# One 32-column strip of the array per quarter of a unit's columns: the decode rows of an input projection on one core

## The chip, the cores and the metric

The kernel runs on one core of a Trainium2 chip. The metric is the device time of one execution in microseconds (us). The core has TensorE (PE, with its weight loads shown apart as PEld), VectorE (DVE), ScalarE (ACT), GpSimd (POOL) and SyncE (SP, which here only issues transfers). The chip grants TensorE a clock that can be lower than the full one; the profile lists the granted share.

## The reference, cut to what matters

A two-branch decoder layer is computed for a prompt of 1024 tokens and, with the same weights, for 8 decode tokens (`x_sample`, one token in each of 8 sequences). What the change touches is the input projection of those 8 rows:

```python
D_MODEL, SEQ, DEC_BATCH = 1024, 1024, 8
SPLIT_SIZES = (W_A, W_A, W_B, W_B, W_B, W_B, W_B, H_B, H_B)     # 7 x 1024 columns, then 2 x 4

def hybrid_layer(x, ...):
    hn = rmsnorm(x, g_norm)
    u = hn @ w_in                                               # (rows, 1024) @ (1024, 7176)
    xa, za, uq, uk, uv, uo, zb, ui, uf = jnp.split(u, SPLIT_IDX, axis=-1)
    k = uk.astype(jnp.float32).reshape(B, S, H_B, DK) * (DK ** -0.5)    # 1/16
    ...

y_prompt, ... = trunk(x_prompt, zero states, weights)           # 1024 rows
y_sample, ... = trunk(x_sample, given states, weights)          # 8 rows
```

## The kernel before, in words

The 7168 wide columns of `w_in` are taken in 14 units of 512 columns, two groups of 256 each (`UNITS`: v0v1, x0y0, q0k0 and so on). A unit's weights lie in two tiles, `raws[u, 0]` for the first 512 rows of `w_in` and `raws[u, 1]` for the last 512, each as 128 partitions x 4 blocks x 512 columns; the 8 blocks of 128 rows are the "blocks of k". `blk(u, a, b)` is the half `a` (256 columns) of tile `b`. `load_raw` fetches a tile in two transfers of 512 KB on SP's queue, one for each half; the next unit's tile goes into the same buffer, so its transfers wait for the last reader of the old one.

For the prompt each unit is multiplied in seven products (a fast scheme on 2x2 blocks, `Q_P1` to `Q_P7`), each of 24 or 48 matmuls, written by `mm3` (lines 66 to 68) as three matmuls on halves of the numbers. These fill TensorE. `prep` makes the operands of a product two products ahead: ScalarE rounds (line 72), VectorE subtracts (line 73). Unit 0 has no such products: its 8 row tiles go through `plain`, while the prompt's rows are still being normalised and transposed (line 442).

The 8 decode rows are multiplied apart, once for each unit, by `dec_unit` (line 251). Its stationary operand is a window of 32 columns of `hnd`: the 8 normalised decode rows of one block of k, transposed, and 24 columns more that nobody reads. Only 32 of the array's 128 columns are needed, and so the array is used as four strips of 32 columns, strip g writing the PSUM partitions 32g to 32g+31. Block k goes to strip k mod 4 and streams all 512 columns of the unit (line 256). Each strip thus holds a partial sum over two blocks of k. ScalarE copies the 128x512 result to `Z` (line 259). Some steps later `turn` transposes its four 128x128 pieces on TensorE (line 264), and VectorE adds the four partial sums while it picks the 8 real rows (line 267), and scales those of a k group by 1/16 (line 269).

A plain float32 matmul is issued as two passes, each with a weight load of its own; so the 8 matmuls of a unit are 16 records in the profile. I call the run of a unit's matmuls its burst.

`dec_unit` is called by `prep` when a unit's fifth-block product (`Q_P5`) is prepared, ahead of the two VectorE steps that overwrite the raw tile in place (lines 281 and 282), and for unit 0 on line 583. Which instruction stands where on an engine is worked out when the kernel is built: a scheduler orders each engine's instructions by its own estimate of when they can start, and each engine then runs its list strictly in that order. For units 0 and 1 the result lies in the PSUM tile `ps_tr`, of which there is one; for the others in `ps_o`, of which there are three.

Of the kernel before, what the change touches and what calls it, by code (L numbers as in the profile page):

```python
# [13 lines left out]
ALU = mybir.AluOpType  # L14
# [3 lines left out]
P = 128  # L18
T = 1024
HT = 512  # L20
NB = 8
KC = 8
# [29 lines left out]
def hymba_kernel(  # L52
# [7 lines left out]
    V, A, G, TE = nc.vector, nc.scalar, nc.gpsimd, nc.tensor  # L60
# [21 lines left out]
    def ps(tag, shape):  # L82
        return psp.tile(shape, F32, tag=tag, name=f"ps_{tag}", bufs=NBUF.get(tag, 1))

    def const(shape, name, dt=F32):
        return cpool.tile(shape, dt, tag=name, name=name)
# [14 lines left out]
    def sg(shape, name, dt=F32):  # L101

        return stg.tile(shape, dt, tag="stg", name=name)
# [4 lines left out]
    def dconst(shape, name):  # L108

        return dpool.tile(shape, F32, tag=name, name=name)  # L110


    idF = const([P, P], "idF")
# [33 lines left out]
    hnd = dconst([P, KC * NB + 24], "hnd")  # L147
# [84 lines left out]
    raws = {}  # L232

    def load_raw(u, b, parts=(0, 1)):
# [5 lines left out]
        for a in parts:  # L240
# [5 lines left out]
    dec_dst = {"q": lambda j: dqk[:, 0, 2 * j:2 * j + 2], "k": lambda j: dqk[:, 1, 2 * j:2 * j + 2],  # L246
               "v": lambda j: dqk[:, 2, 2 * j:2 * j + 2], "o": lambda j: do[:, 2 * j:2 * j + 2],
               "z": lambda j: dz[:, 2 * j:2 * j + 2], "x": lambda j: dxz[:, 0, 2 * j:2 * j + 2],
               "y": lambda j: dxz[:, 1, 2 * j:2 * j + 2]}

    def dec_unit(u):

        pz = ps("tr" if u < 2 else "o", [P, 512])
        for k in range(KC):
            g = k % 4
            TE.matmul(pz[32 * g:32 * g + 32, :], hnd[:, NB * k:NB * k + 32], raws[u, k // 4][:, k % 4, :], start=k < 4, stop=k >= 4,  # L256
                      skip_group_check=True)
        Z = sg([P, 512], "Z")
        A.copy(Z, pz)

        def turn():
            pt = ps("tr", [P, 4, P]) if u < 2 else pz.rearrange("p (m q) -> p m q", m=4)
            for m in range(4):
                TE.transpose(pt[:, m, :], Z[:, m * P:(m + 1) * P], idF)  # L264
            for a, (kind, j) in enumerate(units[u]):
                src = pt[:, 2 * a:2 * a + 2].rearrange("p m (g b) -> p m b g", g=4)[:, :, 0:NB, :]
                V.tensor_reduce(dec_dst[kind](j), src, axis=mybir.AxisListType.X, op=ALU.add)
                if kind == "k":
                    V.tensor_scalar(dec_dst[kind](j), dec_dst[kind](j), 1.0 / 16.0, None, op0=ALU.mult)
        late.append(turn if u < 2 else lambda: late.append(turn))  # L270


# [2 lines left out]
    def blk(u, a, b):  # L275
        return raws[u, b][:, :, a * 256:(a + 1) * 256]

    def prep(u, q):
        if q == Q_P5:
            dec_unit(u)  # L280
            V.tensor_tensor(blk(u, 0, 0), blk(u, 0, 0), blk(u, 1, 0), op=ALU.subtract)
            V.tensor_tensor(blk(u, 1, 0), blk(u, 1, 0), blk(u, 1, 1), op=ALU.add)
        if q == Q_P6:
            V.tensor_tensor(blk(u, 1, 0), blk(u, 1, 1), blk(u, 0, 0), op=ALU.subtract)
        src = {Q_P1: (0, 0), Q_P2: (0, 1), Q_P5: (1, 0), Q_P6: (1, 0), Q_P7: (0, 0), Q_P3: (0, 1), Q_P4: (1, 1)}
        hi, lo = ws([P, 4, 256], f"wh{u}_{q}"), ws([P, 4, 256], f"wl{u}_{q}")
        split(hi, lo, blk(u, *src[q]))
        wops[u, q] = hi, lo
        if q == Q_P6:
            V.tensor_tensor(blk(u, 0, 1), blk(u, 0, 1), blk(u, 1, 0), op=ALU.subtract)  # L290
        b = {Q_P7: 0, Q_P4: 1}.get(q)
        if b is not None:
            if u + 1 < len(units):
                load_raw(u + 1, b)
            else:
                if b == 1:
                    r_open(0)
# [229 lines left out]
    kind, j = units[0][0]  # L527
# [53 lines left out]
    V.tensor_tensor(gd, pgd[0:NB], bgate[0:NB], op=ALU.add)  # L581
    ld(d_gd, gd)
    dec_unit(0)
    load_raw(1, 0)
    load_raw(1, 1)
# [387 lines left out]
    def decode_steps(h):  # L973
# [13 lines left out]
        def token(b):  # L987
# [18 lines left out]
            def products():  # L1006
# [10 lines left out]
                if b == NB - 1:  # L1017
                    Z = sg([P, 256], "qC")
                    V.tensor_copy(Z, pq[:, 0:256])

                    def turn():
                        pt = pq[:, 256:272].rearrange("p (v b) -> p v b", v=2)
                        for vb in range(2):
                            TE.matmul(pt[:, vb, :], Z[:, vb * P:(vb + 1) * P], selq, start=True, stop=True)
                        V.tensor_copy(dqC[:, 2 * h:2 * h + 2, :], pt)
# [803 lines left out]
```

## Time and profile before

| what | value |
|---|---|
| median of 3 runs | 916.23 us (916.17 to 916.24) |
| span of the profiled execution, first to last instruction | 913.5 us |
| its own time beside the span | not listed apart; the median of the runs is 2.7 us above the span |
| mean granted TensorE clock | 0.998 |
| PE, PEld busy | 902.1 us (99%), 749.2 us (82%) |
| DVE, ACT, POOL busy | 741.5 us (81%), 590.1 us (65%), 194.2 us (21%) |
| moved by DMA | 167.68 MB, mean 184 GB/s |
| matmul records | 5259, of them 224 on line 256 and 56 on line 264 |

How to read it: times in the tables below are us from the start of the span; a row of the timeline gives start, length to the end of the last of the merged instructions, engine, line, operation, the tiles out<-in, the part of the array (rows*columns), the shape streamed and the count. Matmuls overlap their neighbours, so how often they start matters more than how long one lasts.

### The profile page before, as it was taken

The page shows a single profiled execution, that of the slowest core. Times are in us where ns is not written, and L with a number is a line of the kernel's source. Part 1 is how long each engine was busy: PE and PEld are TensorE (multiplying, and loading weights), DVE is VectorE, ACT ScalarE, POOL GpSimd, SP SyncE. Part 2 cuts the span into 40 slices and gives each one's busy share as a digit, 9 for nine tenths or more (in the row PEclk, how much of TensorE's full clock was granted, in tenths as well). Part 3 has the DMA queues.
Part 4 walks back from the last instruction along what each step waited for, and adds up shares of the span by engine and source line. Part 5 has one row for each costly group of instructions (what it writes and reads, how often), then busy time and mean ns, then how long its engine had stood idle before and what let it go on. Part 6 is the DMA issues. An engine that isn't in the chain of part 4 may idle for free.

```text
span 913.5 us, 15513 instructions
## 1 busy us (share of the span) xinstructions
PE 902.1 (99%) x5259; PEld 749.2 (82%) x5259; DVE 741.5 (81%) x1532; ACT 590.1 (65%) x1086; POOL 194.2 (21%) x322
## 2 busy tenths in 40 slices
PE   8999999999999999999999999999999999999996
PEld 6897777877787988787789898877788888888886
DVE  6874788978689878789888786679998879888973
ACT  7663446867567776577658786446786568566642
POOL 1111113112312222324332334010111111121120
PEclk9999999999999999999999999999999999999999
DMA  6611457455746566548665747345789889846531
GB/s 202 193 62 46 138 170 243 134 201 186 229 152 212 165 198 198 192 144 265 202 237 167 266 139 243 108 132 188 217 230 260 201 206 300 225 138 183 181 123 68
DMA packets 130488, 167.68 MB, mean 184 GB/s; under 512 B 17596, under 2 KB 98564, under 8 KB 130402
## 3 DMA queue, kind: packets, MB, share of 16 engines
q1 hardware_dynamic: 108790, 103.68, 37.4%
q0 software_dynamic: 21616, 63.02, 21.0%
q8 instruction: 41, 0.67, 0.3%
q14 instruction: 37, 0.30, 0.1%
q10 hardware_dynamic: 4, 0.00, 0.0%
HBM read 108.00 MB, written 62.92 MB: 187 GB/s over the span
## 4 chain that ended last, share of the span: by engine, by line
PE 97%; ACT 1%; DVE 1%; DMA 0%; issue 0%; POOL 0%; ACTq 0%; POOLq 0%
PE ps_o L66 16%; PE ps_o L68 15%; PE ps_o L67 15%; PE ps_kv L66 12%; PE ps_kv L68 11%; PE ps_kv L67 11%; PE ps_o L256 2%; PE ps_s L1195 2%; PE ps_qp L1013 1%; PE ps_s L824 1%; PE ps_tr L824 1%; PE ps_qp L67 1%; PE ps_qp L66 1%; PE ps_qp L68 1%; PE ps_s L1197 1%; PE ps_o L264 1%
## 5 line engine op out<-in xcount | busy, mean ns | idle before, releaser
L72 ACT CAST wh<-raw 128x1024 fp32r<-128x1024 f32 x91 | 95.4, 1049 | 77.9 <-PE ps_o L67 19.3
L73 DVE TENSOR_TENSOR wl<-raw,wh 128x1024 fp32r<-128x1024 f32 x91 | 111.0, 1220 | 34.9 <-ACT wh L72 19.8
L66 PE MATMUL ps_kv<-cb_hi,wh 128*128 128x512 f32 x320 | 127.3, 398 | 0.0
L68 PE MATMUL ps_kv<-cb_hi,wl 128*128 128x512 f32 x320 | 125.3, 392 | 0.0
L67 PE MATMUL ps_kv<-cb_lo,wh 128*128 128x512 f32 x320 | 125.0, 391 | 0.0
L66 PE MATMUL ps_o<-cb_hi,wh 128*128 128x512 f32 x240 | 95.2, 397 | 0.0
L68 PE MATMUL ps_o<-cb_hi,wl 128*128 128x512 f32 x240 | 93.7, 391 | 0.0
L67 PE MATMUL ps_o<-cb_lo,wh 128*128 128x512 f32 x240 | 93.6, 390 | 0.0
L66 PEld LDWEIGHTS ps_kv<-cb_hi,wh 128*128 128x128 f32 x320 | 60.1, 188 | 22.3 <-issue 4.6
L68 PEld LDWEIGHTS ps_kv<-cb_hi,wl 128*128 128x128 f32 x320 | 60.1, 188 | 13.0
L67 PEld LDWEIGHTS ps_kv<-cb_lo,wh 128*128 128x128 f32 x320 | 60.1, 188 | 12.7 <-issue 0.8
L66 PE MATMUL ps_kv<-wh,cb_hi 128*128 128x256 f32 x192 | 55.1, 287 | 0.0
L67 PE MATMUL ps_kv<-wl,cb_hi 128*128 128x256 f32 x192 | 54.4, 283 | 0.0
L68 PE MATMUL ps_kv<-wh,cb_lo 128*128 128x256 f32 x192 | 54.3, 283 | 0.0
L68 PEld LDWEIGHTS ps_o<-cb_hi,wl 128*128 128x128 f32 x240 | 45.1, 188 | 9.9
L66 PEld LDWEIGHTS ps_o<-cb_hi,wh 128*128 128x128 f32 x240 | 45.1, 188 | 9.7 <-issue 0.8
L66 PE MATMUL ps_o<-wo,mh 128*128 128x512 f32 (+1 forms) x136 | 53.0, 390 | 0.0
L67 PEld LDWEIGHTS ps_o<-cb_lo,wh 128*128 128x128 f32 x240 | 45.2, 188 | 8.9
L68 PE MATMUL ps_o<-wo,ml 128*128 128x512 f32 (+1 forms) x136 | 51.7, 380 | 0.0
L67 PE MATMUL ps_o<-wo,mh 128*128 128x512 f32 (+1 forms) x136 | 51.5, 379 | 0.0
L66 PE MATMUL ps_o<-wh,cb_hi 128*128 128x256 f32 x144 | 41.0, 285 | 0.0
L67 PE MATMUL ps_o<-wl,cb_hi 128*128 128x256 f32 x144 | 40.7, 283 | 0.0
(560 smaller groups left out, 2599.8 us busy)
## 6 DMA issues: line engine op xcount, KB each, us to landing
raw<-in_w_in_dram SPq DMA_DIRECT2D x55, 512.0 KB
Cb<-in_state_mlstm_C_dram SPq DMA_DIRECT2D x32, 256.0 KB
out_dram<-Cb POOLq DMA_DIRECT2D x32, 256.0 KB, 4.5
qk<-d_qk SPq DMA_DIRECT2D x32, 256.0 KB
ring<-d_ro SPq DMA_DIRECT2D x26, 256.0 KB
d_qk<-s POOLq DMA_DIRECT2D x24, 256.0 KB, 4.9
d_x<-s POOLq DMA_DIRECT2D x16, 256.0 KB, 2.8
zsr<-d_y SPq DMA_DIRECT2D x16, 256.0 KB
```

What stands on the lines that cost most here:

```text
L66: TE.matmul(out, ah, bh, start=first, stop=False, skip_group_check=True)
L67: TE.matmul(out, ah, bl, start=False, stop=False, skip_group_check=True)
L68: TE.matmul(out, al, bh, start=False, stop=last, skip_group_check=True)
L72: a = A.copy(hi, src)
L73: V.tensor_tensor(lo, src, hi.bitcast(F32), op=ALU.subtract)
L256: TE.matmul(pz[32 * g:32 * g + 32, :], hnd[:, NB * k:NB * k + 32], raws[u, k // 4][:, k % 4, :], start=k < 4, stop=k >= 4, skip_group_chec ...
L264: TE.transpose(pt[:, m, :], Z[:, m * P:(m + 1) * P], idF)
L824: TE.matmul(pg, w[:, n, :], st["xx"][n], start=k == 0, stop=k == 1)
L1013: TE.matmul(pq[32 * g:32 * g + n, 0:256], q, ds_["C", h * NB + bb][:, kb, :], start=b == 1, stop=b == NB - 1, skip_group_check=True)
L1195: TE.matmul(S, qk[:, 2 + kb, :], qk[:, kb, :], start=kb == 0, stop=kb == 1)
L1197: TE.transpose(kn[:, kb * P:(kb + 1) * P], qk[:, 2 + kb, :], idF)
```

## The change

Each strip of the array now takes a quarter of the unit's columns, 128 of them, over all 8 blocks of k, in place of all 512 columns over two blocks. A unit's 8 matmuls of 512 columns become 32 of 128. No partial sums are left to add, the result is 128x128, one transpose turns it, and VectorE only picks and scales the rows (one instruction for each group; the scale is 1 for groups other than k).

```diff
     def dec_unit(u):
-        pz = ps("tr" if u < 2 else "o", [P, 512])
+        pz = ps("tr" if u < 2 else "o", [P, 512])[:, 0:P]
         for k in range(KC):
-            g = k % 4
-            TE.matmul(pz[32 * g:32 * g + 32, :], hnd[:, NB * k:NB * k + 32], raws[u, k // 4][:, k % 4, :], start=k < 4, stop=k >= 4,
-                      skip_group_check=True)
-        Z = sg([P, 512], "Z")
+            for g in range(4):
+                w = blk(u, g // 2, k // 4)[:, k % 4, (g % 2) * P:(g % 2 + 1) * P]
+                TE.matmul(pz[32 * g:32 * g + 32, :], hnd[:, NB * k:NB * k + 32], w, start=k == 0, stop=k == KC - 1,
+                          skip_group_check=True)
+        Z = sg([P, P], "Z")
         A.copy(Z, pz)
 
         def turn():
-            pt = ps("tr", [P, 4, P]) if u < 2 else pz.rearrange("p (m q) -> p m q", m=4)
-            for m in range(4):
-                TE.transpose(pt[:, m, :], Z[:, m * P:(m + 1) * P], idF)
+            pt = ps("tr", [P, 512])[:, 0:P] if u < 2 else pz
+            TE.transpose(pt, Z, idF)
+            rows = pt.rearrange("p (g b) -> p g b", g=4)[:, :, 0:NB]
             for a, (kind, j) in enumerate(units[u]):
-                src = pt[:, 2 * a:2 * a + 2].rearrange("p m (g b) -> p m b g", g=4)[:, :, 0:NB, :]
-                V.tensor_reduce(dec_dst[kind](j), src, axis=mybir.AxisListType.X, op=ALU.add)
-                if kind == "k":
-                    V.tensor_scalar(dec_dst[kind](j), dec_dst[kind](j), 1.0 / 16.0, None, op0=ALU.mult)
+                V.tensor_scalar(dec_dst[kind](j), rows[:, 2 * a:2 * a + 2], 1.0 / 16.0 if kind == "k" else 1.0, None, op0=ALU.mult)
```

In the changed file the matmul stands on line 257, and every line below `turn` stands two lines higher than before. Since the instructions have other shapes and numbers, the scheduler places the first three bursts in another way. From unit 3 on a burst stands undivided where it stood. The places that differ follow. In the names, `raw0_0` and `raw1_0` are the two tiles of unit 0, `raw0_1` and `raw1_1` those of unit 1; `x5`, `x1`, `x3`, `x7` are row tiles of the prompt; `ps_tr_1029` is unit 0's result.

TensorE, the first burst, about 27 us into the span. Before:

```order
L68 MATMUL ps_o_423<-w1h1_292,cb_lo1_190 128x256
L256 MATMUL ps_tr_1029<-raw0_0_219,hnd_112 32x512 x4
L256 MATMUL ps_tr_1029<-raw1_0_232,hnd_112 32x512
L442 MATMUL ps_s_486<-idF_78,x5_300 128x128 x4
L442 MATMUL ps_qp_491<-idF_78,x5_300 128x128 x4
L256 MATMUL ps_tr_1029<-raw1_0_232,hnd_112 32x512 x3
L442 MATMUL ps_kv_577<-idF_78,x1_385 128x128 x2
L66 MATMUL ps_o_515<-wph_211,b12h_496 128x264
```

And now, at the same place:

```order
L68 MATMUL ps_o_423<-w1h1_292,cb_lo1_190 128x256
L257 MATMUL ps_tr_1029<-raw0_0_219,hnd_112 32x128 x13
L440 MATMUL ps_s_486<-idF_78,x5_300 128x128 x4
L440 MATMUL ps_qp_491<-idF_78,x5_300 128x128 x4
L257 MATMUL ps_tr_1029<-raw0_0_219,hnd_112 32x128 x3
L257 MATMUL ps_tr_1029<-raw1_0_232,hnd_112 32x128
L66 MATMUL ps_o_515<-wph_211,b12h_496 128x264
L67 MATMUL ps_o_515<-wpl_212,b12h_496 128x264
L66 MATMUL ps_o_544<-w1h0_288,b12h_496 128x256
L67 MATMUL ps_o_544<-w1l0_289,b12h_496 128x256
L257 MATMUL ps_tr_1029<-raw1_0_232,hnd_112 32x128
L440 MATMUL ps_kv_577<-idF_78,x1_385 128x128 x4
```

Unit 0's burst stood in two pieces (5 and 3 matmuls); its first 18 of 32 now stand in three pieces (13, 4 and 1). Of the other 14, two pieces of 3 stand about 60 us into the span, behind the transposes of `x3`, with two matmuls of `plain` between them, and 8 stand in the next table.

TensorE, where the products of unit 1 begin, about 72 us into the span. Before:

```order
L579 MATMUL ps_o_1017<-wg_213,hnd_112 32x8 x8
L256 MATMUL ps_tr_1058<-raw0_1_1040,hnd_112 32x512 x4
L256 MATMUL ps_tr_1058<-raw1_1_1043,hnd_112 32x512 x4
L66 MATMUL ps_kv_1075<-cb_hi0_187,wh1_0_1050 128x512
L67 MATMUL ps_kv_1075<-cb_lo0_188,wh1_0_1050 128x512
```

And now (the nine matmuls of the first product that follow stand between this table and a piece of 2 on `raw1_1`; after six more follows a piece of 14):

```order
L577 MATMUL ps_o_1017<-wg_213,hnd_112 32x8 x8
L257 MATMUL ps_tr_1029<-raw1_0_232,hnd_112 32x128 x8
L66 MATMUL ps_kv_1123<-cb_hi0_187,wh1_0_1074 128x512
L67 MATMUL ps_kv_1123<-cb_lo0_188,wh1_0_1074 128x512
L257 MATMUL ps_tr_1082<-raw0_1_1064,hnd_112 32x128 x16
L68 MATMUL ps_kv_1123<-cb_hi0_187,wl1_0_1075 128x512
```

Unit 0's last 8 matmuls, the last readers of `raw1_0`, moved to here, and unit 1's burst now comes in pieces of 16, 2 and 14 inside its first product. Unit 2's burst, 4 and 4 around one transpose on line 701 before, now is 13 and 19 around it.

SP's queue of transfers in the same stretch. Before:

```order
L401 DMA x6_476<-in_x_prompt_dram 128x1024
L243 DMA raw0_1_1040<-in_w_in_dram 128x4x256 x2
L401 DMA x2_506<-in_x_prompt_dram 128x1024
L243 DMA raw1_1_1043<-in_w_in_dram 128x4x256 x2
L401 DMA x7_591<-in_x_prompt_dram 128x1024
L401 DMA x3_690<-in_x_prompt_dram 128x1024
L582 DMA d_gd_120<-gd_1026 8x8
L614 DMA dgb_1122<-d_gd_120 128x64
```

And now:

```order
L399 DMA x6_476<-in_x_prompt_dram 128x1024
L399 DMA x2_506<-in_x_prompt_dram 128x1024
L243 DMA raw0_1_1064<-in_w_in_dram 128x4x256 x2
L399 DMA x7_591<-in_x_prompt_dram 128x1024
L399 DMA x3_690<-in_x_prompt_dram 128x1024
L580 DMA d_gd_120<-gd_1026 8x8
L243 DMA raw1_1_1067<-in_w_in_dram 128x4x256 x2
L612 DMA dgb_1164<-d_gd_120 128x64
```

The load of `raw1_1` moved behind two row tiles and behind the small transfer `d_gd`, which is issued after the matmuls of line 577; the load of `raw0_1` moved behind one row tile.

## The prediction

> **What bounds the kernel now.** First the page's busy times and its chain of work that ended last:
>
> ```profile
> PE 902.1 (99%) x5259; PEld 749.2 (82%) x5259; DVE 741.5 (81%) x1532; ACT 590.1 (65%) x1086; POOL 194.2 (21%) x322
> PE 97%; ACT 1%; DVE 1%; DMA 0%; issue 0%; POOL 0%; ACTq 0%; POOLq 0%
> ```
>
> TensorE is the bound: 97% of the chain runs on it. So what the change takes from or adds to TensorE's list counts nearly in full, and what it does to VectorE and ScalarE counts only where TensorE waits for them. Since matmuls overlap, I price them by when the next one starts. Next, the instructions of the two lines that go (name, count, least/median/greatest ns, first and last start), and the timeline of one whole burst and one group of transposes:
>
> ```profile
> L256 PE MATMUL ps_o<-raw,hnd x192: 592/592/617, 115.5 to 612.7; 128*32 128x512 f32 x192
> L264 PE MATMUL ps_o<-idF,Z x48: 270/272/329, 123.9 to 619.5; 128*128 128x128 f32 x48
> ...
> 157.56 0.39 PE L67 MATMUL ps_kv<-cb_lo,wh 128*128 128x512 f32 x1
> 157.79 0.39 PE L68 MATMUL ps_kv<-cb_hi,wl 128*128 128x512 f32 x1
> 158.11 1.92 PE L256 MATMUL ps_o<-raw,hnd 128*32 128x512 f32 x16
> 159.96 0.50 PE L66 MATMUL ps_kv<-cb_hi,wh 128*128 128x512 f32 x1
> ...
> 165.85 0.39 PE L68 MATMUL ps_kv<-cb_hi,wl 128*128 128x512 f32 x1
> 166.08 0.60 PE L264 MATMUL ps_o<-idF,Z 128*128 128x128 f32 x4
> 166.43 0.48 PE L824 MATMUL ps_tr<-xl,ghi 128*128 128x512 f32 x1
> ```
>
> Ordinary matmuls of 512 columns start 0.23 us apart (157.56, 157.79). The burst's 16 passes occupy 1.85 us (158.11 to 159.96). Sixteen passes of 592 ns would take 9.5 us one after the other, so the four strips run side by side and a strip's four passes follow each other. Four transposes last 0.60 us of which the last is 0.272, so they start (0.60 - 0.272) / 3 = 0.109 us apart.
>
> **Price of a narrow pass.** A burst of 128-column passes on strips isn't in the trace. The nearest is line 1013, four strips too, two passes each of 256 columns:
>
> ```profile
> 302.86 0.61 PE L1013 MATMUL ps_qp<-Cb,qsel 128*4 128x256 f32 x8
> 303.41 0.39 PE L66 MATMUL ps_o<-wh,cb_hi 128*128 128x256 f32 x1
> ```
>
> It takes 0.55 us to the next start. If a pass costs in proportion to its columns, with a for 512, and each burst has a fixed part c: 4a + c = 1.85 and 2(a/2) + c = 0.55, so a = 0.433 and c = 0.117. A 128-column pass is then a/4 = 0.108, and the transposes, also float32 of 128 columns, give 0.109. The two rows agree, so I take 0.109. Now each strip has 8 blocks of k x 2 passes = 16 passes: 16 x 0.109 + 0.117 = 1.86 us in place of 1.85.
>
> Bounds: below, nothing, since through each strip pass 2048 columns as before (4 x 512, 16 x 128). Above, the narrowest passes in the trace are those of line 579, 8 columns on one strip:
>
> ```profile
> 71.44 0.28 PE L68 MATMUL ps_o<-w1h,cb_lo 128*128 128x256 f32 x1
> 71.65 0.64 PE L579 MATMUL ps_o<-wg,hnd 128*32 128x8 f32 x15
> 72.12 0.63 PE L256 MATMUL ps_tr<-raw,hnd 128*32 128x512 f32 x3
> 72.15 0.18 PE L579 MATMUL ps_o<-wg,hnd 128*32 128x8 f32 x1
> 73.99 0.50 PE L66 MATMUL ps_kv<-cb_hi,wh 128*128 128x512 f32 x1
> 74.33 0.40 PE L67 MATMUL ps_kv<-cb_lo,wh 128*128 128x512 f32 x1
> ```
>
> The sixteenth starts 0.50 us after the first: 0.033 us each with its weight load, for next to no columns. If that came on top of each of the 12 additional passes of a strip, a burst would cost 0.40 more. I keep 0 and 0.40 as ends; the 256-column row, the nearest, says 0.
>
> The Trainium skill speaks against the change here: "TensorEngine Tiling (Array Packing)", section "Instruction Overhead", gives each matmul some 60 cycles of overhead on trn2 and advises against taking the tiling from a dimension that is already small. Read as an addition to every pass, by its figure and the 2.4 GHz of "TensorE: Matmul & The Clock Gate" it is an estimated 25 ns, 12 x 14 x 0.025 = 4.2 us in all, and the forecast below would become 917.5. The halved price of line 1013's halved passes speaks against that reading.
>
> **What goes for certain.** Three of four transposes in each of 14 units: 14 x 3 x 0.109 = 4.58 us, between matmuls of a saturated TensorE (166.08 to 166.43, with no wait). ScalarE's copy shrinks:
>
> ```profile
> L259 ACT COPY Z<-ps_o x12: 567/588/592, 118.0 to 613.3; 128x512 f32<-128x512 f32 x12
> L518 ACT COPY pe<-ps_o x16: 346/373/374, 16.9 to 71.8; 128x256 f32<-128x256 f32 x16
> L267 DVE TENSOR_REDUCE dqk<-ps_o x10: 211/216/217, 126.5 to 434.5; 128x16 f32<-128x64 f32 x10
> L269 DVE TENSOR_SCALAR dqk<-dqk x4: 165/166/170, 127.9 to 435.2; 128x16 f32<-128x16 f32 x4
> ```
>
> By its two widths a copy of 128 columns is 0.373 - 0.108 = 0.27 us, which saves 14 x 0.32 = 4.5 us of ScalarE. VectorE saves 28 x 0.05 + 4 x 0.166 = 2.1 us. Both lie beside TensorE's work, and I cost them at nothing: if TensorE ran short of operands, part would show as a further gain.
>
> **The bursts that are cut.** Each additional piece costs the change to strips and back: c = 0.12, the entry (157.79 to 158.11 is 0.32, ordinary 0.23: 0.09), and a slow first start after it (73.99 to 74.33 is 0.34, ordinary 0.23: 0.11), together 0.32 us.
>
> - Unit 0: before, 2 pieces and 6 passes on the longest strip, 6 x 0.433 + 2 x 0.32 = 3.24. Now pieces of 13, 4, 1, 3, 3 and 8 have 8, 2, 2, 2, 2 and 4 passes: 20 x 0.109 + 5 x 0.32 + 0.23 (the last follows line 577, already on a strip) = 4.01. That is +0.77. The first piece of 3 falls into a wait that is there now:
>
> ```profile
> 59.34 0.82 PE L442 MATMUL ps_kv<-idF,x 128*128 128x128 f32 x6
> 60.39 0.39 PE L66 MATMUL ps_o<-wph,cb_hi 128*128 128x264 f32 x1 [0.24 <-ACT cb_hi L72]
> ```
>
>   Six transposes need 0.65 us, the next start comes after 1.05: 0.40 is open. Net +0.37.
> - Unit 1: before, 72.12 to 73.99 and 0.11 behind it, 1.98. Now pieces of 16, 2 and 14 have 8, 2 and 8 passes: 18 x 0.109 + 3 x 0.32 = 2.92. +0.94.
> - Unit 2: two pieces before and now; 4 x 0.433 becomes (8 + 10) x 0.109: +0.23.
> - Eleven others: 11 x 0.01 = +0.11.
>
> Sum: -4.58 + 0.37 + 0.94 + 0.23 + 0.11 = -2.93 us, against the span of 913.5, which would be 910.6. The median of the runs lies 2.7 above that span; I leave this distance as it is and forecast 916.23 - 2.93 = **913.3 us**.
>
> **The moved load.** `raw1_1` is now issued only after unit 0's last 8 matmuls. How long a load takes shows where `raw0_1` is loaded (issue on SP; below it, two stretches with their busy times, granted clock, DMA share and GB/s):
>
> ```profile
> 28.37 0.93 SPq L243 DMA_DIRECT2D raw<-in_w_in_dram  x2
> ...
> 28.37:31.00 2.63, 2.63 (x16) 1.01 (x14) 2.54 (x8) 1.23 (x3) 0.21 (x1) 1.00 0.69 181
> 31.00:33.00 2.00, 2.00 (x19) 1.95 (x17) 1.83 (x3) 1.36 (x3) 0.00 (x0) 1.00 1.13 386
> ```
>
> 2.63 us x 181 GB/s = 476 KB of the first half's 524; the rest takes 0.12, so the first half is there 2.75 us after the issue, the second 1.36 later. Counting from the start of line 577: the 8 matmuls end at about 1.07, the load is issued at 1.15, halves land at 3.9 and 5.3. TensorE meanwhile has two matmuls, the piece of 16 and nine matmuls, and comes to the piece of 2 (first half) at 4.95 and to the piece of 14 (second half) at 6.9. ScalarE and VectorE then have 1.05 and 1.22 us of work on the first half for the second product, due at 9.6. Nothing waits, with 1.0 us to spare; beyond that each us late costs one on TensorE, and behind the waiting piece stands the rest of unit 1's first product. `dgb` behind it on SP is used some 4 us after its issue, and slips by one. Were `raw1_1` there earlier, nothing would be gained.
>
> **The rivals.**
>
> 1. The start costs more than summed (within 0.2%). The 0.40 us of cover is missing since the pieces move PE and ScalarE together, and the load takes 4.7 us instead of 2.75, 1.0 beyond its slack: -2.93 + 0.40 + 1.0 = -1.5, 914.7. For it: the order was made by estimates, and the margin is 1 us. Against: the loads' rate above, and transfers are few at that place.
> 2. Each narrow pass pays a fixed price on top of its columns (the tiling page's rule is of this kind). At 0.033, 14 x 0.40 = 5.6: 913.3 + 5.6 = 918.9, slower; below 0.028 it ends within 0.2%. Against: line 1013, and a strip's weights load while its other pass streams.
> 3. TensorE isn't fed. A whole burst now is 64 passes with 64 weight loads in 1.86 us, 29 ns a pair. From 29 ns on each further ns costs 64 x 14 = 0.9 us; from 32 ns the gain is gone, and at 36 ns the time is 913.3 + 6.3 = 919.6, slower. For it: the densest run in the trace, line 579's, has 33 ns a pair, and only for 16 pairs. Against: all these pairs are on one strip, where they queue for each other, and those of line 256 behind them start three at once. "TensorE: Matmul & The Clock Gate", section "Wait — 56ns, not 53.3ns?", states about 62 ns per matmul where the sequencer decodes in microcode; line 579's 33 ns show that this isn't the case here.
>
> **How the numbers follow.** A measurement of this kernel tells about 0.2%, 1.8 us, from no change. Forecast case, -2.93 with an own range of 911.7 (all cuts of the start hidden) to 914.4: 0.68. Rival 1: 0.18. Rival 2: 0.08, half of it within 0.2%. Rival 3: 0.06. So faster 0.68, same 0.18 + 0.04 = 0.22, slower 0.04 + 0.06 = 0.10. The range reaches from 911.7 over the first rival into the lower prices of the second, 916.6.
>
> **What would show it.** Right: a burst from unit 3 on takes 1.85 to 1.90 us to the next start; line 264's successor has 14 records; the new group of units 0 and 1 costs about 1.3 us more in all before 82 us of the span, and from there on the lead over the kernel before grows by 0.3 us a unit. Wrong: bursts over 2.0 us, a wait of TensorE for `raw1_1` near 76 us, or a lead that is lost again behind 620 us, where the code is the same.

## The result and the profile after

The changed kernel takes 914.6 us (median of 21 runs, 913.23 to 915.59); the kernel before took 915.99 beside it (21 runs, 915.12 to 916.60). The ratio is 0.9983, 95% interval 0.9977 to 0.9988: faster by 1.4 us, about half of the 2.9 that were forecast. I read the profile in the same order as that of before. First the page's busy times and the shares of the chain:

```profile
PE 899.7 (99%) x5889; PEld 762.1 (83%) x5889; DVE 739.3 (81%) x1528; ACT 585.2 (64%) x1086; POOL 194.8 (21%) x322
PE 30%; DVE 2%; ACT 1%; issue 0%
```

TensorE's busy time fell by 2.4 us, and the span by 0.7 (913.5 to 912.8). The 0.7 is less than the medians have, since the trace of before is one of its shorter executions: in the later series the median span of its runs is 914.0 to 914.2 us. The chain could be followed over a third of the span only, so its shares say less than before. Next, in the timeline, the burst of unit 3, and the one transpose that is left of four with what stands around it:

```profile
158.68 0.39 PE L68 MATMUL ps_kv<-cb_hi,wl 128*128 128x512 f32 x1
158.99 1.95 PE L257 MATMUL ps_o<-raw,hnd 128*32 128x128 f32 x64
160.88 0.50 PE L66 MATMUL ps_kv<-cb_hi,wh 128*128 128x512 f32 x1
...
166.72 0.39 PE L68 MATMUL ps_kv<-cb_hi,wl 128*128 128x512 f32 x1
166.95 0.27 PE L264 MATMUL ps_o<-idF,Z 128*128 128x128 f32 x1
166.98 0.47 PE L822 MATMUL ps_tr<-xl,ghi 128*128 128x512 f32 x1
```

From the start of the matmul ahead to the start of the one behind, the burst takes 2.20 us (158.68 to 160.88) where it took 2.17 (157.79 to 159.96): 64 narrow passes cost 0.03 us more than 16 wide ones. From the matmul ahead of the transposes to the one behind it is 0.26 us in place of 0.58. From its first start to the next matmul's the burst takes 1.88 us in all eleven units from 3 on, and the saving on the transposes is 0.33 us in each. At the start, unit 1's load comes late:

```profile
76.00 0.39 PE L67 MATMUL ps_kv<-cb_lo,wh 128*128 128x512 f32 x1
76.58 0.41 PE L257 MATMUL ps_tr<-raw,hnd 128*32 128x128 f32 x4 [0.19 <-DMA raw<-in_w_in_dram]
76.92 0.50 PE L68 MATMUL ps_kv<-cb_hi,wl 128*128 128x512 f32 x1
```

The bracket is TensorE's wait for `raw1_1`, 0.19 us, ahead of the piece of 2. And the waits of TensorE over the whole span (us in total, times, longest) hold, from 70 us on, five that the kernel before did not have: these four, at 474, 630, 534 and 77 us, and one of 0.2 us at 673:

```profile
PE ps_kv L66 <- ACT c L353: 1.0, 1, 1.0
...
PE ps_s L1071 <- DVE dworkb L1069: 0.4, 1, 0.4
...
PE ps_s L822 <- DVE xh L816: 0.3, 1, 0.3
...
PE ps_tr L257 <- DMA raw<-in_w_in_dram: 0.2, 1, 0.2
```

Where the gain comes and goes is best seen by taking one instruction that stands in both kernels and subtracting its start in the trace of before from that in the trace of another kernel; negative is a lead. The head row gives the places, by their time in the trace of before; the last column is each kernel's span (before: 913.5). The first place lies just ahead of unit 2's burst. The expectations below take their 0.7 from 110.4 us, where the changed kernel stands at +0.68; but around there two small matmuls (lines 659 and 660 of before) come three matmuls later in its list, and once both kernels have them behind them the lag is 0.85.

| place in the trace of before, us | 115.2 | 124.3 | 299.4 | 389.5 | 398.2 | 433.3 | 478.0 | 619.5 | 677.3 | 762.0 | span |
|---|---|---|---|---|---|---|---|---|---|---|---|
| changed | +0.85 | +0.75 | -0.35 | -0.93 | -0.91 | -1.16 | -0.45 | -0.79 | -0.63 | -0.55 | 912.8 |
| changed, second execution | +0.97 | +0.87 | -0.24 | -0.81 | -0.80 | -1.07 | -1.38 | -1.92 | -1.15 | -0.90 | 912.3 |
| wide start | +0.15 | +0.05 | -0.79 | -1.36 | -1.29 | -1.42 | -1.74 | -2.31 | -1.02 | -0.93 | 912.5 |
| wide start, load freed | -0.14 | -0.25 | -0.88 | -1.46 | +0.11 | -0.01 | -0.32 | -0.51 | -0.38 | +0.70 | 914.0 |
| wide start, no stores | -0.03 | -0.13 | +0.05 | -0.53 | +0.25 | +0.15 | -0.16 | -1.01 | +0.01 | +1.35 | 914.6 |
| narrow start alone | +0.98 | +1.74 | +1.74 | +1.74 | +1.73 | +1.72 | +1.72 | +1.90 | +3.31 | +3.32 | 916.8 |
| four transposes | +1.41 | +1.64 | +1.85 | +1.91 | +1.91 | +1.97 | +3.03 | +3.19 | +3.67 | +4.30 | 917.5 |
| changed, no stores | +1.06 | +0.96 | +0.06 | -0.52 | -0.51 | -0.72 | -0.72 | -1.56 | -1.56 | -1.09 | 912.2 |
| before, no stores | -0.05 | -0.04 | -0.04 | -0.04 | -0.04 | -0.06 | -0.06 | -0.06 | +0.18 | +0.16 | 913.6 |

Row two is, up to 619 us, what the prediction describes: late by 1 us at first, then ahead by some 0.3 us more for each unit. Row one is the same up to 433 us and then loses 1.0 us in one step at 474 us and 0.5 in another at 534, with the gains of the units between them. The other rows are the experiments below.

The wait on line 1071, at 630 us, is of another kind than the rest. TensorE loses 0.28 to 0.31 us there in all nine profiled executions that have the change in units 2 to 13 with TensorE's list at that place as in the changed kernel, whether it is 2.3 us ahead of before (wide start), 3.2 behind (opposite order) or 16.3 behind (loads on POOL's queue). In the trace of before and in the second execution VectorE works from 616 us to there without a wait for a load. Its lead over before is 1.57 us at 616 us and 1.62 at 629 us, while TensorE's grows from 1.59 to 1.92 by unit 13's transposes at 619 us. So TensorE comes 0.3 us too early for `dworkb`: what the change saves in unit 13 is lost again, by the order of the instructions and not by a transfer.

### The profile page after: what moved, and what is told of

Read it like the earlier page. It is cut to its first block, busy times and chain, and to the rows that moved or that the text cites. A ratio compares the mean times of both kernels' runs of the same rounds, so it can differ in the third digit from the quotient of the medians.

```text
span 912.8 us, 16738 instructions
## 1 busy us (share of the span) xinstructions
PE 899.7 (99%) x5889; PEld 762.1 (83%) x5889; DVE 739.3 (81%) x1528; ACT 585.2 (64%) x1086; POOL 194.8 (21%) x322
```

## The experiments

Each kernel was timed in five rounds (the one with 64 columns in three) beside the kernel before on the same chip, so the ratios to it are what can be compared across groups. I began with theory A (the start ate the missing part), against B (TensorE's lead is taken from it at fixed places).

**Wide bursts in units 0 and 1, the change in units 2 to 13.**

```diff
     def dec_unit(u):
+        (dec_unit_wide if u < 2 else dec_unit_narrow)(u)     # wide: as before
```

> Units 0 and 1 go back to the 512-column bursts of before with four transposes each; units 2 to 13 keep the narrow bursts and the single transpose. Theory A (the gain of the later units stands, and the cut bursts of the start are what it lost): units 0 and 1 give back the 0.7 us by which the changed kernel's trace is late at 110 us of the span, less the 6 x 0.11 = 0.65 us that their six additional transposes cost and that are in those 0.7 already; so 0.7 us under the changed kernel, 913.9. Theory B (the lead of TensorE is taken from it at fixed places, 474, 534 and 630 us, where it waits for ScalarE and VectorE, whatever it had before): the lead at 433 us is 1.9 instead of 1.2, the wait at 474 grows by the same 0.7, and the time stays at 914.6.

Measured: 916.24 us (914.38 to 917.31), ratio 0.9998 (0.9989 to 1.0007). Neither theory has this: not the 0.7 us less of A, not the same time of B, but the time of before. Yet its profiled execution, the fastest of its eleven, is 0.8 us ahead of the changed kernel's second one at 124 us and 0.4 at 619 us. What was to be had at the start was there in this execution; by the median the typical one did not keep it.

**Narrow bursts in units 0 and 1 alone.**

```diff
+        (dec_unit_narrow if u < 2 else dec_unit_wide)(u)
```

> The kernel before, with the narrow bursts and single transposes in units 0 and 1 alone. Theory A: 0.7 us more than before, 916.7, and the trace is 0.7 late from 110 us to the end. Theory B: the delay is absorbed at the places where TensorE waits for the other engines, and the time is that of before within 0.3, 916.0.

Measured: 919.07, ratio 1.0029 (1.0017 to 1.0040), 2.9 us more than before. The start itself is 0.80 late at 110 us, where A had read its 0.7, and 0.98 at 115 us. Three things come on top. Unit 2's burst was now cut into 5 and 3 matmuls, not 4 and 4, as the timeline shows (before: 115.52, 116.59, 116.85):

```profile
116.50 1.91 PE L256 MATMUL ps_o<-raw,hnd 128*32 128x512 f32 x10
118.33 0.33 PE L723 MATMUL ps_qp<-idF,stk 128*128 128x128 f32 x1
118.59 1.06 PE L256 MATMUL ps_o<-raw,hnd 128*32 128x512 f32 x6
```

With 5 matmuls one strip has four passes ahead of line 723 instead of two: 1.83 us to the next start in place of 1.07, and the lag goes to 1.74. It then stays at 1.74 for 350 us: nothing absorbs a delay of TensorE, which is against B. The second addition, 0.9 us, is at 630 us, and the third, 0.5, at 677. VectorE's timeline at 630 us:

```profile
630.59 1.23 DVE L1401 TENSOR_TENSOR ws<-wc,wc 128x1024 f32<-128x1024 f32 x1 [0.82 <-DMA wc<-in_w_out_dram]
631.73 0.22 DVE L1092 SCALAR_TENSOR_TENSOR dworkb<-do,dworkb 128x64 f32<-128x64 f32 x1
```

VectorE stands 0.82 us for a load of `wc`, and the small decode steps on `dworkb`, for which TensorE waits next (0.98 us at 633.37), stand behind it in VectorE's list.

**Four transposes again in the changed kernel.**

```diff
-            TE.transpose(pt, Z, idF)
+            for m in range(4):
+                TE.transpose(pt, Z, idF)
```

> The changed kernel with each unit's one transpose issued four times into the same place, so with the 3 x 14 = 42 transposes again that the change removed (the result of the last is used, the value is the same). Theory A: 42 x 0.109 = 4.6 us more, 919.2, and above the kernel before by the whole price of the narrow bursts, 3.2 us. Theory B: 0.33 us a unit delays TensorE by 3.3 us at 474 us, so that its waits there (1.0 us), at 534 (0.3) and at 630 (0.4) fall away, and the time grows by 4.6 - 1.7 = 2.9 only, to 917.5.

Measured: 920.18, ratio 1.0042 (1.0029 to 1.0056). Against the changed kernel's own ratio (0.9982 in its second series) that is 5.5 us more, and 4.7 by the spans (917.5 to 912.8): A's 4.6, not B's 2.9. So a transpose that is taken out of TensorE's list is worth its 0.109 us (4.7 / 42 = 0.112 by the spans). The row of the table also gives the burst's price by itself, since the transposes now cancel: from 166 to 389 us of before, five units, the lag grows from 1.78 to 1.91, 0.03 a unit. And it holds a surprise. This TensorE is 3.1 us behind the changed kernel's at 433 us, and its list of waits still has the one at 474 us:

```profile
PE ps_kv L66 <- ACT c L354: 1.0, 1, 1.0
```

So that wait does not come from TensorE being early: here it is 2.0 us later than in the trace of before, which has no such wait.

**The start's bursts in the opposite order.**

```diff
+        at = [(k, g) for k in range(KC) for g in range(4)]
+        if u < 2:
+            at.reverse()
```

> The changed kernel with the bursts of units 0 and 1 taken in the opposite order (last block of k first, second half of the columns first), so that they begin when the block that arrives last is there. By the order of the instructions the start then has four stretches on strips (16, 4, 12 and 16 together, 16 matmuls) instead of eight, with 32 passes on the longest strip instead of 38. Theory A: 32 x 0.11 + 4 x 0.32 = 4.8 us against 38 x 0.11 + 8 x 0.32 = 6.7 less the 0.4 that lay in a wait; 1.1 to 1.5 us under the changed kernel, 913.1 to 913.5, and the wait for the moved load near 76 us is gone. Theory B: this lead is lost at 474 us like the rest, 914.6. A third way: TensorE waits near 60 us for the second block instead, by more than the stretches cost, and the time is above 914.6.

Measured: 919.86, ratio 1.0037 (1.0024 to 1.0049): the third way, at another place than I named. Unit 0's first block is now read last, so the buffer for unit 1's first block comes free last. Its load is issued at 71.67 us, and TensorE's waits show the price:

```profile
PE ps_kv L66 <- ACT wh L72: 3.9, 1, 3.9
...
PE ps_s L1074 <- DVE dworkb L1072: 0.4, 1, 0.4
```

The second line is the wait at 630 us again, in a kernel whose TensorE is 3.2 us behind.

**The changed kernel again, and one load set free.** What these runs had in common were waits that followed a transfer. In the next group the changed kernel ran again for a second profile, and the last load of `wc`, for which the kernel with the wide start had waited 0.56 us at 642 us, no longer waited for two stores.

> The changed kernel itself once more, beside the others on the same chip, as their yardstick and for a second profiled execution. Expected by all theories: 914.6 within 0.5. If the waits of TensorE at 474, 534 and 630 us are in its order of instructions, they stand in this execution too, with 1.0, 0.3 and 0.4 us; if they come from transfers that land later or earlier, they differ.

Measured: 914.46 (913.09 to 915.25), ratio 0.9982 (0.9973 to 0.9991). The wait at 474 us is absent. ScalarE's timeline shows where the two executions part; first the changed kernel, then its second execution:

```profile
463.47 0.72 ACT L990 ACTIVATE Cb<-Cb,dGI 128x512 f32<-128x512 f32 x1 [3.67 <-DMA d_qk<-s]
464.10 0.80 ACT L836 ACTIVATE rg<-rg,sp4n 128x512 f32<-128x512 f32 x1
...
473.86 0.59 ACT L353 COPY c<-ps_kv 128x512 f32<-128x512 f32 x1
```

```profile
462.40 0.73 ACT L990 ACTIVATE Cb<-Cb,dGI 128x512 f32<-128x512 f32 x1 [2.52 <-DMA Cb<-in_state_mlstm_C_dram]
463.03 0.80 ACT L836 ACTIVATE rg<-rg,sp4n 128x512 f32<-128x512 f32 x1
...
472.80 0.59 ACT L353 COPY c<-ps_kv 128x512 f32<-128x512 f32 x1
```

`Cb` is a state matrix that the decode steps load, scale and store. ScalarE waits for transfers in both and starts 1.07 us later in the first. The first bracket names `d_qk`, a transfer that landed at the same moment; but in the second execution ScalarE starts 1 us before `d_qk` lands, so what it needs is the load of `Cb`. A transfer has 16 marks of landing in the trace, and this load has its last at 463.38 and 462.31 us, 0.09 us ahead of ScalarE in both. It was issued at 453.98 and 453.41 us (in the first 0.08 us behind the last mark of a load of `raw`) and took 9.4 and 8.9 us. ScalarE's list is the same in both, so all behind it is 1.06 us later, down to the copy `c` that frees the PSUM buffer `ps_kv`, which TensorE's next product needs:

```profile
474.50 0.39 PE L66 MATMUL ps_kv<-wh,cb_hi 128*128 128x256 f32 x1 [0.96 <-ACT c L353]
```

So the step of row one begins with a transfer, eleven microseconds ahead of TensorE's wait. The kernel with the load of `wc` set free, which takes `nrow` from the staging buffers:

```diff
-        nrow = mx["pn"].tile([64, 512], F32, tag="nrow", name="nrow")
+        nrow = sg([64, 512], "nrow")
```

> The changed kernel with the row nrow taken from the staging buffers instead of a pool of its own, whose memory the last of the four loads of wc takes over: so this load no longer waits for the two stores of nrow (in the changed kernel's trace it is issued at 637.3 us, TensorE needs it at 643.05, and such a load took 5.4 us in the kernel with wide bursts at the start, where TensorE waited 0.6 us for it). Theory C (what TensorE has gained by 620 us is partly given back between 630 and 680 us, where it comes to loads that are issued behind stores and VectorE's work): the load comes earlier, 0.3 to 1 us are gained, 913.6 to 914.3. Otherwise: 914.6.

Measured: 914.86 (913.83 to 915.72), ratio 0.9986 (0.9977 to 0.9995): no gain over the 0.9982 of the changed kernel. In its profiled execution the step came elsewhere: ScalarE waited 1.4 us for loads of `Cb` near 129 us (0.9 and 0.8 in the two executions of the changed kernel), and TensorE lost 0.6 us at 133 us.

> The kernel with wide bursts in units 0 and 1 (which had a lead of 2.3 us over the kernel before at 619 us of its profiled execution, 1.0 at the end of it, and none in the median of its runs, 916.2), and nrow in the staging buffers. Theory C, with the wait for the last load of wc as the main place: this load is no longer late in any execution, the 0.6 us of the profiled execution and the more of the others come back, 914.0 to 914.8. If the lead is lost in other places of that stretch (the loads of ring, near 677 us) or before it: 915.5 to 916.2.

Measured: 915.82 (914.47 to 917.71), ratio 0.9992 (0.9983 to 1.0001). That is 0.4 us better than without the free load by the medians and 0.5 by the ratios, inside the uncertainty. Theory C is not it: the loss is not at one load. This profiled execution is a typical one of its series, and it loses 1.57 us at 398 us. ScalarE's timeline has the reason, first in the kernel with the wide start, then in this one (the lists of ScalarE are the same up to there):

```profile
374.39 1.05 ACT L72 CAST wh<-raw 128x1024 fp32r<-128x1024 f32 x1 [4.75 <-DMA raw<-in_w_in_dram]
```

```profile
375.80 1.05 ACT L72 CAST wh<-raw 128x1024 fp32r<-128x1024 f32 x1 [6.26 <-DMA raw<-in_w_in_dram]
```

The weights of unit 8, issued at 368.16 and 368.06, let ScalarE begin 6.2 and 7.7 us later. The half of them that it reads first has its last mark of landing at 374.29 and 375.70 us, 0.1 us ahead of ScalarE; in the second kernel 15 of the 16 marks are there by 372.94. The 1.41 us stay on ScalarE's list until 399 us, and TensorE, 1.46 us ahead, meets it:

```profile
398.26 0.50 PE L66 MATMUL ps_o<-cb_hi,wh 128*128 128x512 f32 x1 [1.40 <-DVE s L355]
```

**Narrower still, 64 columns from unit 3 on.** Part of the decode rows' sums is lost in this kernel; the instructions are those that the expectation names.

> The changed kernel, and in units 3 to 13 each matmul of 128 columns is issued as two of 64, so 128 passes with 128 weight loads in a burst and 32 on each strip. If a pass costs in proportion to its columns, and TensorE takes a pair of load and pass in 14 ns: the burst stays at 1.88 us, 914.6. If each pass has a fixed price on top, 0.033 us as the upper end of the prediction: 16 x 0.033 x 11 = 5.8 us more, 920.4. If TensorE takes no more than one pair in some 25 ns: 128 x 0.025 = 3.2 us a burst, 15 us more, 929.

Measured: 919.15, ratio 1.0030 (1.0018 to 1.0043). The timeline of a burst:

```profile
158.60 0.39 PE L68 MATMUL ps_kv<-cb_hi,wl 128*128 128x512 f32 x1
158.92 2.07 PE L258 MATMUL ps_o<-raw,hnd 128*32 128x64 f32 x128
160.92 0.50 PE L66 MATMUL ps_kv<-cb_hi,wh 128*128 128x512 f32 x1
```

128 pairs of load and pass go in 2.00 us to the next start, against 1.88 for 64: 0.11 us for 16 more passes on each strip, 7 ns each, and 11 x 0.11 = 1.2 us in all. The other two prices are ruled out for the burst. The time rose by 4.5 us nevertheless: this order of instructions has waits of TensorE for ScalarE's `s` and `c` of 1.7 and 1.6 us, which I did not take further.

**Less traffic.** Theory D: it is the landing of loads that takes the lead away, through ScalarE's and VectorE's lists. It was tried by leaving the 32 stores of `Cb` out of three kernels, against E (the order of instructions takes it).

```diff
-                stq(s_C[0, b, h].rearrange("(kb p) v -> p kb v", p=P), C)
```

> The changed kernel without the 32 stores of the new states Cb (this output is left out). Theory D: each execution is like its best ones (913.1 to 913.8), a median of 913.5 to 914.2 and a spread under 1.5 us. Theory E: 914.5 with a spread of 2.2.

Measured: 914.0 (913.48 to 914.53), ratio to the whole kernel before 0.9977 (0.9967 to 0.9987). As D has it, in the median and in the spread, 1.05 us where the whole changed kernel has 2.2 to 2.4. But of the 0.5 us between this median and that of the changed kernel's second series (914.46) only 0.25 lies in the spans (912.25 and 912.5 by their medians), and the intervals of the two ratios overlap. No step of 0.5 us or more is left in its row of the table before 619 us; steps of 0.3 us are, at 133 and 475 us.

> The kernel before without the 32 stores of the new states Cb (this output is left out), the yardstick of the two others. Its TensorE waited for nothing between 120 and 620 us of the profiled execution although ScalarE waited 22.8 us for loads of Cb and 11 for loads of raw. Theory D: it gains little, 915.7 to 916.1, and the changed kernel without the stores is 2.0 to 2.5 us faster than this one. Theory E: 916.1, and the distance stays at 1.6.

Measured: 915.18 (914.77 to 916.23), ratio 0.9989 (0.9980 to 0.9997). This gains 0.8 us where D had 0.1 to 0.5, so the distance to the changed kernel is 1.2 us, and not the 2.0 to 2.5 that D promised: the change gains no more with less traffic than with all of it. The runs of this kernel too lie closer together, 1.5 us where those of before in the same series have 3.2. Its row also says how exact such a table is: from 115 to 619 us it repeats the trace of before within 0.06 us.

> The kernel with wide bursts in units 0 and 1, without the 32 stores of the new states Cb to the output (256 KB each, 8 MB; this output is left out), so fewer transfers beside the loads of Cb and of raw. Theory D (in the executions in which a load of Cb or of raw lands a microsecond or two late, ScalarE's list waits for it, and TensorE, which now runs 1 to 2 us ahead, waits in turn; with less traffic such executions are rare): it keeps the lead of 2.3 us that its best execution had at 619 us, of which about 1 us is lost behind 630 us; 914.2 to 914.9, with runs closer together than the 2.9 us of before. Theory E (its lead is lost by the order of the instructions, not by transfers): 916.2, spread as before.

Measured: 915.35 (914.12 to 916.39), ratio 0.9989 (0.9980 to 0.9998). D is wrong here: 0.5 to 1.1 us over it, and still wide in spread. Its profiled execution is the slowest of its series, and shows what remains: TensorE loses 1.0 us at 133 us, 0.8 at 398 us again (behind the same load of `raw`, which is late with the stores left out too), and 2.4 between 630 and 762 us. TensorE's waits there:

```profile
PE ps_qp L67 <- DVE Cl L73: 1.0, 1, 1.0
...
PE ps_qp L1323 <- ACT hh L1272: 0.8, 1, 0.8
...
PE ps_tr L1389 <- DMA wc<-in_w_out_dram: 0.4, 1, 0.4
```

The last is a load by name. In front of the first, ScalarE waited 1.5 us for a load of `oraw`, until 758 us. So D has one of the three medians and E none. By the ratios the stores cost the kernel before 1.0 us, the changed one 0.5 and the one with the wide start 0.8, the first alone clear of the uncertainty: they cost the changed kernels no more than the other, so their traffic does not account for what the change fell short of.

**The loads of Cb on POOL's queue.**

```diff
-            ld(t, st_C[0, b, h].rearrange("(kb p) v -> p kb v", p=P))
+            stq(t, st_C[0, b, h].rearrange("(kb p) v -> p kb v", p=P))
```

> The changed kernel with the loads of Cb issued on POOL's queue instead of SP's, where they stand behind the loads of raw; the order of TensorE's instructions stays as it is. Theory D: the loads of Cb are issued when their buffer is free, ScalarE's waits for them (11 to 18 us in the changed kernel's two traces) shrink, and with them the executions with a wait of TensorE: 913.8 to 914.3. Rival: they stand behind stores in POOL's queue now, or the 16 DMA engines are the limit whatever the queue: 914.5 or more.

Measured: 932.65, ratio 1.0183 (1.0165 to 1.0202): the rival, by far. In the waits of ScalarE:

```profile
ACT Cb L990 <- DMA Cb<-in_state_mlstm_C_dram: 38.0, 12, 6.0
```

38.0 us in place of 13.6 and 17.6 in the two executions of the changed kernel, and TensorE waits up to 7.3 us at a time. In POOL's list the loads stand behind stores that wait for VectorE (56.6 us in all for the stores `d_p` alone). The Trainium skill, "DMA: Bandwidth & Descriptors", section "SWDGE vs HWDGE vs iDMA", gives plain transfers to the queues of SP or ACT and leaves to GpSimd those that accumulate or cast; this run agrees, with the 38.0 us, though it cannot tell the queue's order from the cost of issuing there.

## Why the prediction came out as it did

The sign, the large terms of the sum and the range were right; the forecast lay 1.3 us low. By the line that the prediction drew itself, 1.8 us, a gain of 1.4 is not told from no change, so of its three outcomes this one is "same" (0.22) and not "faster" (0.68); that the gain is there all the same, the 21 runs beside 21 tell. The steps, as changes of the lag over each stretch, with the second execution in the last column:

| stretch, us of before | forecast | changed | again |
|---|---|---|---|
| to 115: units 0 and 1 | +0.66 | +0.85 | +0.97 |
| 115 to 124: unit 2 | -0.10 | -0.10 | -0.10 |
| 124 to 433: units 3 to 9 | -2.22 | -1.91 | -1.94 |
| 433 to 619: units 10 to 13 | -1.27 | +0.37 | -0.85 |
| 619 to 762 | 0 | +0.24 | +1.02 |

- **Transposes.** Right: 0.33 us a unit in the trace, and the kernel with four transposes gives the 4.6 us back.
- **Price of a narrow pass.** Right: 1.88 us to the next start where 1.86 was forecast, so +0.03 for a unit and not +0.01, 0.2 us over eleven. 12 more passes on a strip cost 0.03 us, 16 further ones of 64 columns 0.11 (3 and 7 ns each). The rule weighed against it, some 60 cycles of overhead for each matmul by "TensorEngine Tiling (Array Packing)" of the Trainium skill, section "Instruction Overhead", is not what these runs show if it is read as an addition to every pass. Rival 2 falls with the 3 ns, and rival 3 with the 64 pairs in 1.88 us.
- **The cut bursts.** Right, but for the moved load. TensorE waited 0.19 and 0.32 us for it, one of the signs of being wrong that I had named, and the lags of 0.85 and 0.97 us less these waits are 0.66 and 0.65: the pieces cost what they were priced at. The load was mis-sized. It was to leave 1.0 us to spare, with its first half there 2.75 us after the issue; its last mark of landing came 3.93 us after it (72.60 to 76.53). The load from whose GB/s the 2.75 was worked out has its own last mark 3.84 us after its issue, in the trace of before. Unit 2's burst cost 0.23 as forecast (lag 0.85 to 1.08).
- **The step that failed** is "what the change takes from or adds to TensorE's list counts nearly in full", drawn from TensorE's 97% of the chain. It held for what was added: the lag of the narrow start alone stays at 1.74 us for 350 us. For what was taken away the sum lacks a term, the waits that TensorE does not have in the trace of before. One of them, 0.3 us at 630 us, is there in every execution, since VectorE's list did not become shorter with TensorE's. The others come in some executions and not in others. In the units each of the 0.3 us was gained (166 to 389 us: 0.294 a unit in the second execution), but single steps of 0.3 to 1.6 us took several units' gain back. Each of these that I followed (not the 0.5 us at 534 us of the first execution, nor 0.3 at 500 us of the second) began with ScalarE or VectorE waiting for a load (`Cb`, `raw`, `wc`, `oraw`). They do not need a lead: the two kernels that are late by 1.9 and 2.0 us lost 0.9 at 630 us and 1.0 at 474 us in the same way. The trace of before had a sign of them that I did not read: ScalarE's waits between 100 and 620 us.

```profile
ACT Cb L992 <- DMA Cb<-in_state_mlstm_C_dram: 22.8, 13, 3.5
ACT wh L72 <- DMA raw<-in_w_in_dram: 11.0, 3, 4.8
```

  Not one of these 34 us reached TensorE in that execution, which waited for nothing between 120 and 620 us. I had costed ScalarE's savings at nothing because TensorE hid them, and did not ask how much slack was left where the loads come in. How long such waits are does not tell it: in the changed kernel's first execution the same two rows are 13.6 (17.3 with the wait that its view puts to `d_qk`) and 9.9 us, less than before, and 1.3 us of waiting reached TensorE.
- **Behind 620 us**, where I had named a lost lead as a sign against me, the second execution gave back 1.0 of its 1.9 us, of which 0.3 at 630 (the one that is always there), 0.5 at 677 and 0.25 up to 762 us.
- **Rival 1** has the time (914.7) but not the way: the start cost 0.2 to 0.3 us more than summed up to 124 us, not 1.4.
- **The tally.** Losses that are in both executions: 0.2 to 0.3 us for the moved load, 0.2 for the bursts of eleven units, 0.3 at 630 us, so 0.7 to 0.8 of the 1.3. The rest lies in the waits that differ between executions. The kernel before has them too: the 2.7 us that the prediction put beside its span are 2.0 (the runs' times less their spans, by the median) and 0.5 to 0.7 by which its traced execution was shorter than the median one. How the rest divides over the places stays open.

What is shown: that the wait at 474 us follows ScalarE's longer wait for transfers, since it comes and goes between two executions of one kernel, and stays in a kernel whose TensorE is 3 us later; that the loss at 630 us comes with the change, whatever TensorE's lag; and that without the stores the runs of all three kernels lie closer together. That transfers took the rest of the missing gain is argued from the steps that were followed and not shown, since without the stores the change gains 1.2 us, not more than with them. What stays open: why the wide start, whose profiled execution (the fastest of its series) leads the changed kernel's second one by 0.4 to 0.8 us up to 619 us, ends 1.1 to 1.5 us behind it by the ratios, with stores and without. In three profiled executions of such kernels the loss stood at 133, 398 and 630 to 762 us, behind loads where I could follow it. Whether a larger lead makes a load land later for that kernel, or only leaves less slack for it, none of the runs tells apart. No variant that computes all outputs beats the changed kernel.

## What to carry to other kernels

In this kernel, where TensorE has 99% of the span, time added to its list was paid at least in full, but of the 2.9 us that should have been taken from it about half was kept, because the lists of the other engines did not become shorter with it. So look, before counting a gain, at two things: which list runs without a pause up to an instruction that the bounding engine needs next (there the gain ends at once), and which lists wait for loads on their own (there it ends in the executions in which a load lands late). And for gains of a microsecond, take a second profile of the same kernel: a step that is in one and not in the other does not come from the order of the instructions, and one that is in all of them, however early or late TensorE is, hardly comes from a late transfer.

## What the runs showed of the hardware that I had not expected

- TensorE took a pair of weight load and 64-column pass every 14.5 ns on four strips (128 pairs, 1.847 us from the first start to the last), where the changed kernel's burst has 26.7 ns (64 pairs, 1.68 us), at a granted clock of 0.998.
- The kernel before and the one without stores agree to 0.06 us on TensorE from 115 to 619 us, where no late load reached TensorE in either; the two executions of the changed kernel part in single steps, of 1.0 us at 474 us and 0.5 at 534.
- Half of the weights of unit 8 (512 KB), issued at 368.1 us in two kernels whose ScalarE lists are alike up to there, let its reader start 6.2 us later in one and 7.7 in the other. In the second, 15 of the 16 marks of landing were there 4.9 us after the issue, and the last 2.8 us behind them.
